# Feed-forward matmuls of a two-layer encoder: from the full array to two 64-row tiles

## The chip, the cores and the metric

One core of a Trainium2 chip runs the whole program in one launch. The metric is device time in microseconds; the kernel before takes 1270.34 us (median of three runs, 1270.18 to 1270.63).

## What is computed

Two encoder layers over 256 tokens of width 1024, in float32. Each layer is a feed-forward half step, a mixer of three attention branches, and a second feed-forward half step:

```python
def swiglu(h, w1, w3, w2):
    return (jax.nn.silu(h @ w1) * (h @ w3)) @ w2
for l in range(DEPTH):                       # DEPTH = 2
    x = x + 0.5 * swiglu(rms_norm(x, ffn1_norm[l]), ffn1_w1[l], ffn1_w3[l], ffn1_w2[l])
    ...                                      # the mixer
    x = x + 0.5 * swiglu(rms_norm(x, ffn2_norm[l]), ffn2_w1[l], ffn2_w3[l], ffn2_w2[l])
```

w1 and w3 are 1024 x 2816, w2 is 2816 x 1024. So there are four feed-forward blocks, and the change touches nothing else.

## The kernel before

**Split products.** TensorE takes float32r operands. To keep float32 accuracy every operand a is split into hi = round(a) and lo = a - hi, and a product is summed as hi*hi + hi*lo + lo*hi. Activations are kept transposed: `xT[:, t, w, k, :]` holds tokens of half t (128 each), w = 0 for hi and 1 for lo, for feature block k.

**The weight stream.** All weights come in units of up to 1 MB, in a fixed order (L74 to L111). A unit goes by DMA from SP's queue into one of three `raw` buffers (L115), ScalarE rounds it to hi in two halves (`emit_hi`, L133, the instruction on L138), VectorE subtracts to get lo (`emit_lo`, L141, the instruction on L144), both into one of four `hl` buffers. `unit()` (L157) hands out the next unit and writes out the splits that are still missing up to the first half of the one behind it; `tick()` (L181), called between bursts of matmuls, writes out the next splits (`fill`, L163, at most two units ahead) and lets each side task take a step. The order of the program text is the order in each engine's queue.

**A feed-forward block** (`ffn`, L448) has 22 units of w1 and w3 (128 columns of each, eight blocks of 128 rows) and then 11 units of w2.
- Units 0 and 1 run with the activations as the stationary operand (`tform`, L451) while the norm is still being finished; their results are transposed by `tr_task` (L462). In the first block of the program `start_first` (L298) does these two units instead.
- Units 2 to 21 run through `fform` (L493): for b = 0 (w1) and b = 1 (w3), and for each of eight k, one matmul with hi weights streams 512 columns (hi and lo of the 256 tokens, L503), and one with lo weights streams 256 columns (hi, L504). The two halves of a PSUM bank collect xhi*whi + xhi*wlo and xlo*whi apart. `rs_bcast` (L290) transposes the norm factors over all partitions after unit 2.
- `fdrain` (L473) evacuates a unit: per bank a ScalarE copy of the upper half (L478) and a VectorE add of the lower (L479), a GpSimd multiplication by the norm factor (L480), then SiLU, gate product and split (L485 to L491).
- `wide_out` (L413) multiplies by w2: for each of the first nine units and each token half t, `wide_burst` (L437) issues 12 matmuls of 512 columns into two banks. Units 9 and 10 are held to the end, so that each of the four banks is finished in turn.

Eight PSUM banks: four tagged `acc`, four tagged `ta` (L69 to L71). `fform` uses two `acc` banks a unit; `wide_out` uses all four.

## Time and profile before

| what | value |
|---|---|
| runs | 1270.34 us median (1270.18 to 1270.63) |
| profiled execution, first to last instruction | 1267.6 us |
| granted TensorE clock | 1.000 over the whole span |
| PE busy / weight loads busy | 1253.1 us / 1074.4 us |
| VectorE / ScalarE / GpSimd busy | 894.0 / 711.9 / 221.3 us |
| read from HBM | 224 MB, 178 GB/s over the span |

The profile gives the span of its execution, not a time of its own beside it; the median of the runs is 2.7 us more than that span, which is what lies ahead of the first and behind the last instruction. Matmuls are pipelined: a row's "busy" overlaps the next one's, so that the pace of TensorE is read from starts and counts, not from durations. "PEld" is the weight load that precedes each matmul.

### The profile page before, as it was taken

To read this page: it belongs to the slowest core of one execution; us is meant where nothing else is said; L and a number is where in the kernel's file an instruction comes from. 1 tells how busy PE (TensorE), PEld (TensorE's weight loads), DVE (VectorE), ACT (ScalarE), POOL (GpSimd) and SP (SyncE) were. 2 spreads that over 40 slices of the span, in tenths; PEclk is the share of its full clock that TensorE was granted. 3 is DMA by queue.
4 is the path that set the end of the run, shared out by engine and by line. 5 is a ranking of instruction groups with operands and counts; after the bars stand their busy time and mean duration, and the time that the engine had idled before them with its cause. 6 is when DMAs were issued, how large, how long until landed. Compare 5 with 4: busy or idle time off the path is not lost.

```text
span 1267.6 us, 18330 instructions
## 1 busy us (share of the span) xinstructions
PE 1253.1 (99%) x7124; PEld 1074.4 (85%) x7124; DVE 894.0 (71%) x1382; ACT 711.9 (56%) x1315; POOL 221.3 (17%) x169
## 2 busy tenths in 40 slices
PE   8999999999999999999999999999999999999998
PEld 7888788889988898888898888888899788988887
DVE  5888736678766878886378886466886567788852
ACT  6555536667665366555365564356686644665541
POOL 0322101132011112220012220021322020122200
PEclk9999999999999999999999999999999999999999
DMA  7655644552543545556355556346526434555561
GB/s 301 222 180 187 241 158 158 203 194 87 196 166 133 200 166 185 185 196 232 133 186 203 195 195 235 113 173 225 167 90 207 163 134 170 196 199 182 186 230 34
DMA packets 37751, 228.34 MB, mean 180 GB/s; under 512 B 5712, under 2 KB 6864, under 8 KB 13088
## 3 DMA queue, kind: packets, MB, share of 16 engines
q1 hardware_dynamic: 37488, 227.09, 50.5%
q8 instruction: 56, 0.92, 0.3%
q14 instruction: 31, 0.25, 0.1%
q0 software_dynamic: 32, 0.07, 0.0%
q10 hardware_dynamic: 144, 0.00, 0.0%
HBM read 224.00 MB, written 1.05 MB: 178 GB/s over the span
## 4 chain that ended last, share of the span: by engine, by line
PE 88%; DVE 7%; ACT 4%; issue 1%; DMA 0%; DVEq 0%; ACTq 0%
PE acc L368 79%; DVE hl L144 6%; PE ta L368 6%; ACT hl L138 2%; ACT s L478 1%; PE ta L689 1%; PE ta L259 1%; DVE s L487 1%; PE ta L776 0%; DVE aT L1017 0%; PE ta L1172 0%; DMA gcol<-in_gcol 0%; PE ta L674 0%; ACT aT L1016 0%; PE ta L608 0%
## 5 line engine op out<-in xcount | busy, mean ns | idle before, releaser
L144 DVE TENSOR_TENSOR hl<-raw,hl 128x1024 fp32r<-128x1024 f32 (+2 forms) x422 | 568.0, 1385 | 101.7 <-ACT hl L138 91.4
L138 ACT ACTIVATE hl<-raw 128x1024 fp32r<-128x1024 f32 (+2 forms) x422 | 417.2, 1041 | 110.2 <-PE acc L368 93.5
L368 PE MATMUL acc<-xT,hl 128*128 128x512 f32 (+1 forms) x2768 | 475.6, 334 | 0.6 <-DVE s L479 0.6
L368 PEld LDWEIGHTS acc<-xT,hl 128*128 128x128 f32 x2768 | 417.8, 188 | 55.7 <-DVE s L479 0.9
L368 PE MATMUL acc<-hl,xT 128*128 128x512 f32 (+2 forms) x1728 | 369.0, 369 | 0.0
L368 PEld LDWEIGHTS acc<-hl,xT 128*128 128x128 f32 x1728 | 299.8, 188 | 45.7 <-issue 2.1
L368 PE MATMUL acc<-hl,s 128*128 128x512 f32 x1344 | 310.9, 391 | 1.5 <-DVE s L479 1.5
L368 PEld LDWEIGHTS acc<-hl,s 128*128 128x128 f32 x1344 | 250.8, 188 | 54.4 <-DVE s L479 1.9
L480 POOL TENSOR_TENSOR s<-s,rsb 128x512 f32<-128x512 f32 x80 | 111.8, 1397 | 355.7 <-DVE s L479 355.7
L489 ACT ACTIVATE s<-s 128x256 fp32r<-128x256 f32 x82 | 34.2, 418 | 172.4 <-DVE s L487 172.4
L479 DVE TENSOR_TENSOR s<-acc,s 128x256 f32<-128x256 f32 x158 | 59.6, 419 | 58.5 <-ACT s L478 58.5
L569 POOL TENSOR_TENSOR sm<-sm,mhalf 128x4 f32<-128x4 f32 (+2 forms) x24 | 36.7, 1531 | 202.7 <-DVE sm L573 196.0
L280 POOL TENSOR_TENSOR sm<-sm,mhalf 128x1 f32<-128x1 f32 x12 | 14.2, 1182 | 298.5 <-DVE sm L279 298.5
L478 ACT ACTIVATE s<-acc 128x256 f32<-128x256 f32 x158 | 50.6, 372 | 0.0
L242 ACT ACTIVATE s<-ta 128x512 fp32r<-128x512 f32 (+1 forms) x46 | 22.9, 531 | 39.9 <-PE ta L689 19.9
L243 DVE TENSOR_TENSOR s<-ta,s 128x512 fp32r<-128x512 f32 (+1 forms) x46 | 26.6, 604 | 24.4 <-ACT s L242 24.1
L368 PE MATMUL ta<-s,s 64*64 64x128 f32 (+3 forms) x720 | 41.0, 265 | 2.1 <-ACT s L1026 2.1
L368 PEld LDWEIGHTS ta<-s,s 64*64 64x64 f32 (+2 forms) x720 | 32.1, 144 | 12.4 <-issue 5.9
L262 ACT ACTIVATE xT<-ta,gain 128x128 fp32r<-128x128 f32 x80 | 22.8, 369 | 35.1 <-PE ta L259 35.1
L485 ACT ACTIVATE s<-s 128x256 f32<-128x256 f32 x82 | 34.2, 418 | 10.9 <-POOL s L480 0.2
L546 DVE SCALAR_TENSOR_TENSOR x<-acc,x 128x512 f32<-128x512 f32 (+1 forms) x20 | 11.3, 579 | 39.7 <-PE acc L368 39.7
L491 DVE TENSOR_TENSOR s<-s,s 128x256 fp32r<-128x256 f32 x82 | 34.0, 415 | 1.9 <-ACT s L489 1.9
(158 smaller groups left out, 652.4 us busy)
## 6 DMA issues: line engine op xcount, KB each, us to landing
raw<-in_l_f_w SPq DMA_DIRECT2D x130, 1024.0 KB, 4.8
raw<-in_l_in_g SPq DMA_DIRECT2D x16, 816.0 KB, 4.4
raw<-in_l_in_late SPq DMA_DIRECT2D x8, 1024.0 KB, 4.8
raw<-in_l_out SPq DMA_DIRECT2D x8, 1024.0 KB, 4.7
raw<-in_l_in_m SPq DMA_DIRECT2D x4, 1024.0 KB, 4.8
raw<-in_l_in_gr SPq DMA_DIRECT2D x4, 1024.0 KB, 4.8
raw<-in_l_in_r SPq DMA_DIRECT2D x4, 1024.0 KB, 4.8
raw<-in_l_in_nv SPq DMA_DIRECT2D x4, 1024.0 KB, 5.0
```

Source lines behind the costliest of these rows:

```text
L138: ACT.activation(out=hls[j][:, 0, sl], in_=raws[j][:, sl], func=AF.Copy)
L144: DVE.tensor_tensor(out=hl[:, 1, sl], in0=r[:, sl], in1=hl[:, 0, sl].bitcast(F32), op=ALU.subtract)
L242: ACT.activation(out=hi, in_=ps, func=AF.Copy)
L243: DVE.tensor_tensor(out=lo, in0=ps, in1=hi.bitcast(F32), op=ALU.subtract)
L368: PE.matmul(out=out, lhsT=lhsT, rhs=rhs, start=start, stop=stop, skip_group_check=True)
L478: ACT.activation(out=g[:, j, :], in_=a[j][:, 256:], func=AF.Copy)
L479: DVE.tensor_tensor(out=g[:, j, :], in0=a[j][:, :256], in1=g[:, j, :], op=ALU.add)
L480: POOL.tensor_tensor(out=g, in0=g, in1=rb[:, None, :].to_broadcast([128, 2, 256]), op=ALU.mult)
L485: ACT.activation(out=g[:, 0, :], in_=g[:, 0, :], func=AF.Silu)
L489: ACT.activation(out=o[:, 0, :], in_=g[:, 0, :], func=AF.Copy)
L491: DVE.tensor_tensor(out=o[:, 1, :], in0=g[:, 0, :], in1=o[:, 0, :].bitcast(F32), op=ALU.subtract)
L569: POOL.tensor_tensor(out=r[:, :n], in0=ss[:, :n], in1=mhalf[:, :n], op=ALU.pow)
```

## The change

`duo` is new. It takes two lists of runs, P and Q. A run is a list of matmuls into one PSUM bank. Each 128-row matmul is cut in two of 64 rows (`HALF`), and the matmuls of P on one half of the rows alternate with those of Q on the other half. After both runs of P and Q are through on their first halves, the halves are exchanged. Since both halves add into the same bank, a GpSimd memset of one element (`dot`) waits for the ends of a pair of first runs, and the pair of second runs into those banks waits for that memset.

`fform_pair` does two units of w1/w3 at a time: P and Q are the two units, with two runs (w1, w3) of 24 matmuls of 256 columns each (three per k), all into one sum of 256 columns. Their four banks alternate between `ta` and `acc`. `fdrain` is then called with both banks as a and b, which leaves out L478, L479 and L480 and multiplies straight from PSUM by the norm factor (L483, L484). In `wide_out`, P and Q are the two token halves, with two runs of six matmuls of 512 columns; the held units stay as they were. The first block keeps `fform` for units 2 and 3. `tr_task` is now finished right behind `rs_bcast` after the first pair.

```diff
+        def duo(P, Q, between=None):
+            gate = {}
+            for second in (False, True):
+                for n, pair in enumerate(zip(*((Q, P) if second else (P, Q)))):
+                    last = [None, None]
+                    for i in range(len(pair[0][0])):
+                        for r in range(2):
+                            ops, start, stop = pair[r]
+                            out, lhsT, rhs = ops[i]
+                            last[r] = mm(out, lhsT[HALF[r]], rhs[HALF[r]], start and not second and i == 0,
+                                         stop and second and i == len(ops) - 1)
+                            if second and i == 0:
+                                tc.add_manual_dep(last[r], gate[n], SYNC, reason="the other row tile's run in this bank")
+                    if not second:
+                        g = POOL.memset(dot[:, n:n + 1], 0.0).ins
+                        for r in range(2):
+                            tc.add_manual_dep(g, last[r].name, SYNC, reason="both row tiles' runs")
+                        gate[n] = g.name
+                    if between is not None and not (second and n == len(P) - 1):
+                        between()
...
@@ wide_out
-                for t in range(2):
-                    if u == 0:
-                        accs[t] = (acc_t(), acc_t())
-                    wide_burst(accs[t], lhs, u, hl, t, u == 0, False)
-                    tick()
+                if u == 0:
+                    for t in range(2):
+                        accs[t] = (acc_t(), acc_t())
+                P, Q = (wide_runs(accs[t], lhs, u, hl, t) for t in range(2))
+                duo(*((Q, P) if u % 2 else (P, Q)), between=tick)
+                tick()
...
+        def wide_runs(acc, lhs, u, hl, t):
+            runs = []
+            for h in range(2):
+                ops = []
+                for kk in range(2):
+                    sl = slice(kk * 1024 + h * 512, kk * 1024 + h * 512 + 512)
+                    for x_, w_ in ((0, 0), (0, 1), (1, 0)):
+                        ops.append((acc[h], lhs(x_, u, kk, t), hl[:, w_, sl]))
+                runs.append((ops, u == 0, False))
+            return runs
...
+            def fform_pair(i):
+                runs, accs = [], []
+                for j in (i, i + 1):
+                    hl = unit()
+                    acc = [at_t() if i // 2 % 2 == 0 else acc_t() for _ in range(2)]
+                    accs.append(acc)
+                    runs.append([])
+                    for b in range(2):
+                        o = acc[b][:, :256].rearrange("p (t n) -> p t n", t=2)
+                        ops = []
+                        for k in range(8):
+                            a = k * 256 + b * 128
+                            for w_, x_ in ((0, 0), (0, 1), (1, 0)):
+                                ops.append((o, hl[:, w_, a:a + 128], xT[:, :, x_, k, :]))
+                        runs[-1].append((ops, True, True))
+                duo(*runs, between=tick)
+                if i == 2:
+                    rs_bcast()
+                    finish(utr)
+                for j in range(2):
+                    drains[i + j] = run(fdrain(i + j, accs[j][0][:, :256], accs[j][1][:, :256]))
+                tick()
...
-            for i in range(2, NB):
-                fform(i)
+            if first is not None:
+                for i in (2, 3):
+                    fform(i)
+            for i in range(2 if first is None else 4, NB, 2):
+                fform_pair(i)
```

How the instructions move on TensorE in the w1/w3 stage: of before, a stretch of one unit (`xT` is the moving operand, `hl` the weights; 512 and 256 are columns):

```order
L368 MATMUL acc<-xT,hl 128x256
L368 MATMUL acc<-xT,hl 128x512 [waits DVE_49]
L368 MATMUL acc<-xT,hl 128x256
L368 MATMUL acc<-xT,hl 128x512
L368 MATMUL acc<-xT,hl 128x256
```

Of the change, one pair of units (the size shown is the output's, all 128 partitions of it; each of these matmuls takes 64 rows):

```order
L367 MATMUL acc<-xT,hl 128x256 [waits Activation_49] x2
L367 MATMUL acc<-xT,hl 128x256 x2
L367 MATMUL acc<-xT,hl 128x256 [waits DVE_49] x2
L367 MATMUL acc<-xT,hl 128x256 x19
L367 MATMUL acc<-xT,hl 128x256 [waits Activation_49]
L367 MATMUL acc<-xT,hl 128x256 x3
L367 MATMUL acc<-xT,hl 128x256 [waits DVE_49]
L367 MATMUL acc<-xT,hl 128x256 x66
L367 MATMUL acc<-xT,hl 128x256 [waits Pool_49]
L367 MATMUL acc<-xT,hl 128x256 x47
L367 MATMUL acc<-xT,hl 128x256 [waits Pool_49]
L367 MATMUL acc<-xT,hl 128x256 x47
```

Before, two units were 64 matmuls; now they are 192, of 256 columns and 64 rows each, in four stretches of 48, the third and fourth of which begin with a wait for GpSimd.

TensorE in the w2 stage of the change, from the middle of a unit's first stretch to its end (s_396 and s_520 are the split gate products of two 128-column blocks):

```order
L367 MATMUL acc<-hl,s_520 128x512 [waits Activation_49]
L367 MATMUL acc<-hl,s_520 128x512
L367 MATMUL acc<-hl,s_520 128x512 [waits DVE_49]
L367 MATMUL acc<-hl,s_520 128x512 x3
L367 MATMUL acc<-hl,s_396 128x512 x6
L367 MATMUL acc<-hl,s_520 128x512 x6
L367 MATMUL acc<-hl,s_396 128x512 [waits Pool_49]
L367 MATMUL acc<-hl,s_396 128x512 x5
L367 MATMUL acc<-hl,s_520 128x512 x6
L367 MATMUL acc<-hl,s_396 128x512 [waits Pool_49]
L367 MATMUL acc<-hl,s_396 128x512 x5
L367 MATMUL acc<-hl,s_520 128x512 x6
```

A unit was 24 matmuls of 128 rows; it is 48 of 64 rows, again in four stretches, of 12 matmuls each, and the third and fourth begin with the wait for GpSimd.

GpSimd in the first block, before:

```order
L280 TENSOR_TENSOR sm<-sm,mhalf 128x1 [waits DVE_49]
L480 TENSOR_TENSOR s_335<-s_335,rsb 128x512 [waits DVE_49]
L480 TENSOR_TENSOR s_397<-s_397,rsb 128x512 [waits DVE_49]
L480 TENSOR_TENSOR s_449<-s_449,rsb 128x512 [waits DVE_49]
L219 MEMSET aT_78 128x512
L219 MEMSET aT_79 128x512
```

and with the change:

```order
L512 TENSOR_TENSOR s_398<-s_398,rsb 128x512 [waits DVE_49]
L393 MEMSET dot 1x1 [waits PE_49] x2
L218 MEMSET aT_78 128x512
L218 MEMSET aT_79 128x512
L393 MEMSET dot 1x1 [waits PE_49,Pool_49] x34
```

The multiplications of the drains are gone but for those of units 2 and 3, and 34 memsets follow each other, each behind matmuls.

## Rows read from the trace of the kernel before

**Rows 1.** The page: busy time by engine, granted clock in 40 slices
```profile
PE 1253.1 (99%) x7124; PEld 1074.4 (85%) x7124; DVE 894.0 (71%) x1382; ACT 711.9 (56%) x1315; POOL 221.3 (17%) x169
...
PEclk9999999999999999999999999999999999999999
```

**Rows 2.** The page: the chain that ended last, by engine
```profile
PE 88%; DVE 7%; ACT 4%; issue 1%; DMA 0%; DVEq 0%; ACTq 0%
```

**Rows 3.** Waits of PE (us in total, times, longest)
```profile
PE ta L368 <- ACT hl L337: 6.0, 1, 6.0
PE ta L368 <- ACT s L1026: 2.1, 2, 1.1
PE acc L368 <- DVE s L479: 2.1, 2, 1.5
PE ta L1172 <- DVE s L1163: 0.4, 2, 0.2
```

**Rows 4.** Windows in the second block's w1/w3 and w2 stages: length, busy (instructions)
```profile
475.00:570.00 95.00, 95.00 (x543) 83.24 (x542) 79.85 (x104) 55.70 (x102) 23.75 (x17) 1.00 0.55 189
580.00:618.00 38.00, 38.00 (x169) 31.47 (x168) 20.70 (x20) 16.28 (x17) 0.00 (x0) 1.00 0.61 224
```

**Rows 5.** Groups by form, 475 to 570 us (busy us, mean ns | idle before)
```profile
L368 PE MATMUL acc<-xT,hl 128*128 128x512 f32 x271 | 95.2, 393 | 0.0
L368 PE MATMUL acc<-xT,hl 128*128 128x256 f32 x272 | 76.9, 283 | 0.0
L144 DVE TENSOR_TENSOR hl<-raw,hl 128x1024 fp32r<-128x1024 f32 x36 | 58.2, 1655 | 2.7 <-ACT hl L138 0.4
...
L480 POOL TENSOR_TENSOR s<-s,rsb 128x512 f32<-128x512 f32 x17 | 23.8, 1397 | 70.6 <-DVE s L479 70.6
L479 DVE TENSOR_TENSOR s<-acc,s 128x256 f32<-128x256 f32 x34 | 12.8, 419 | 12.9 <-ACT s L478 12.9
```

**Rows 6.** Groups by form, 580 to 618 us
```profile
L368 PE MATMUL acc<-hl,s 128*128 128x512 f32 x169 | 38.5, 389 | 0.0
...
L144 DVE TENSOR_TENSOR hl<-raw,hl 128x1024 fp32r<-128x1024 f32 x18 | 22.0, 1270 | 17.0 <-ACT hl L138 16.8
```

**Rows 7.** The chain, 276 to 320 us: start, us, what
```profile
279.67 2.80 PE acc L368 x12
282.46 0.87 PE ta L689 x8
...
307.62 2.85 PE acc L368 x24
```

**Rows 8.** Timeline of row-tiled loads, then matmuls, of the latent attention, cut to windows
```profile
296.33 0.19 PEld L368 LDWEIGHTS ta<-s,s 64*128 64x128 f32 x2
296.33 0.30 PEld L368 LDWEIGHTS ta<-s,s 64*128 64x128 f32 x4
296.33 0.42 PEld L368 LDWEIGHTS ta<-s,s 64*128 64x128 f32 x6
296.55 0.41 PE L368 MATMUL ta<-s,s 64*128 64x256 f32 x4
```

**Rows 9.** Groups by form, PE and PEld, whole span
```profile
L368 PE MATMUL ta<-s,s 64*128 64x256 f32 x48 | 5.0, 312 | 0.0
...
L368 PEld LDWEIGHTS acc<-hl,s 128*128 128x128 f32 x1344 | 250.8, 188 | 54.4 <-DVE s L479 1.9 <-issue 0.7
L368 PEld LDWEIGHTS ta<-s,s 64*128 64x128 f32 x48 | 3.4, 185 | 1.1
```

**Rows 10.** Timeline of four 64 x 64 tiles (linear attention), windows ended one round later
```profile
380.11 0.56 PE L368 MATMUL ta<-s,s 64*64 64x128 f32 x12
380.11 0.67 PE L368 MATMUL ta<-s,s 64*64 64x128 f32 x16
```

**Rows 11.** The chain around the 64 x 64 tiles, 378 to 388 us
```profile
380.78 2.97 PE acc L368 x12
383.75 0.82 PE ta L368 x24
```

**Rows 12.** Groups by form, POOL, whole span: the smallest memset
```profile
L300 POOL MEMSET ones<- 128x1 f32 x1 | 0.1, 98 | 0.0
```

More of the change, by code (lines that the diff above doesn't have):

```diff
@@ L28 @@
 S2_BUFS = 31
-FIRST_R = 2
 ROW = {}
@@ L367, in mm @@
         def mm(out, lhsT, rhs, start, stop):
-            PE.matmul(out=out, lhsT=lhsT, rhs=rhs, start=start, stop=stop, skip_group_check=True)
+            return PE.matmul(out=out, lhsT=lhsT, rhs=rhs, start=start, stop=stop, skip_group_check=True).ins
+        HALF = (slice(0, 64), slice(64, 128))
+        dot = cst.tile([1, 4], F32, name="dot")
+        SYNC = mybir.DependencyInfo(mybir.DependencyClass.Sync, mybir.DependencyReason.DATA)
+        def duo(P, Q, between=None):
[18 more added lines that the diff above has]
+                        between()
         def burst(acc, lh, hl, ks, t, N, start, stop, k0=0):
@@ L435, in wide_out @@
                     tick(True)
-        def wide_burst(acc, lhs, u, hl, t, start, stop):
-            for kk in range(2):
-                s, e = start and kk == 0, stop and kk == 1
-                for w in range(2):
-                    for h in range(2):
-                        mm(acc[h], lhs(0, u, kk, t), hl[:, w, kk * 1024 + h * 512:kk * 1024 + h * 512 + 512],
-                           s and w == 0, False)
-                for h in range(2):
-                    mm(acc[h], lhs(1, u, kk, t), hl[:, 0, kk * 1024 + h * 512:kk * 1024 + h * 512 + 512], False, e)
+        def wide_runs(acc, lhs, u, hl, t):
[8 more added lines that the diff above has]
+            return runs
         def ffn(norms, after, prefetch, first=None, out=None):
@@ L494, in fform @@
                 hl = unit()
-                acc = [(at_t() if first is not None and i == 3 else acc_t()) for _ in range(2)]
+                acc = [(at_t() if i == 3 else acc_t()) for _ in range(2)]
                 for b in range(2):
@@ L504, in fform @@
                         tick()
-                if i == (FIRST_R if first is not None else 2):
+                if i == 2:
                     rs_bcast()
-                    if first is not None:
-                        for j in range(2):
-                            drains[j] = run(fdrain(j, first[j][0][:, :256], first[j][1][:, :256]))
-                        for j, a in held:
-                            drains[j] = run(fdrain(j, a))
-                if "x" in rs_b:
-                    drains[i] = run(fdrain(i, acc))
-                else:
-                    held.append((i, acc))
-                tick()
-            us, drains, held = {}, {}, []
+                    for j in range(2):
+                        drains[j] = run(fdrain(j, first[j][0][:, :256], first[j][1][:, :256]))
+                drains[i] = run(fdrain(i, acc))
+                tick()
+            def fform_pair(i):
[14 more added lines that the diff above has]
+                duo(*runs, between=tick)
+                if i == 2:
+                    rs_bcast()
+                    finish(utr)
+                for j in range(2):
+                    drains[i + j] = run(fdrain(i + j, accs[j][0][:, :256], accs[j][1][:, :256]))
+                tick()
+            us, drains = {}, {}
             if first is None:
@@ L526, in ffn @@
                         tick(t == 0)
-                utr = spawn(tr_task(us), 2)
-            for i in range(2, NB):
-                fform(i)
+                utr = spawn(tr_task(us), 99)
+            if first is not None:
[3 more added lines that the diff above has]
+                fform_pair(i)
                 if i == 4:
@@ L533, in ffn @@
                         load_consts()
-                    if first is None:
-                        finish(utr)
             def lhs(hl, u, kk, t):
```

## Prediction

> **What bounds the kernel now.** [...] Busy PE is not yet PE at its pace, so the next view is what PE waits for: 10.6 us in all, of which 6.0 us at the start, and 2.1 us behind the drains of w1/w3 in the feed-forward [rows 3]. TensorE is bound by its own instruction stream; only a shorter stream helps.
>
> Its pace comes from counts. Of the records that touch a window, about two began before it. In the w1/w3 stage 95 us hold some 541 starts [rows 4], half of them of 512 and half of 256 columns [rows 5]: 0.1756 us each, 5.62 us for a unit's 32 matmuls and **11.24 us for two units**. In the w2 stage 38 us hold some 167 starts [rows 4], all of 512 columns [rows 6]: **0.227 us each**. [...]
>
> **The change, part by part.**
>
> *w1/w3 in pairs.* A unit's columns stay the same (512 + 256 become 256 + 256 + 256), but three loads take the place of two in each k. A pair of units becomes 96 slots, each of two half-height matmuls side by side. If both tiles of a slot run at once, a pair costs 96 slots. The latent attention already has this very form: float32r, 64 rows, 128 weight columns, 256 moving columns, 48 records [rows 9], in two tiles. Its loads cover 0.19 us for the first two, 0.30 us for four and 0.42 us for six [rows 8]: the two tiles begin within 0.01 us (one load lasts 0.185 us [rows 9]), and the third slot adds 0.12 us. The last four matmuls cover 0.41 us [rows 8], of which the last alone is some 0.28 us (the full-array form has 0.283 [rows 5]), which leaves 0.13 us for one slot and the lag of the second tile. So the tiles do run at once, and a slot takes 0.12 us, rounded; I take 0.119, as the full array has it at 256 columns. Hence 96 x 0.119 = 11.42 us against 11.24: +0.18 us a pair. There are 9 pairs in the first block and 10 in each of the others, 39 in all: **+7.2 us**. The bounds of a slot are 0.109 us, the step of one round of the four 64 x 64 tiles (0.67 - 0.56 = 0.11 [rows 10]), and 0.13 us, the upper end of the rounding; each 0.005 us is worth 96 x 39 x 0.005 = 18.7 us.
>
> *w2 in tiles.* 24 slots of 512 columns take the place of 24 matmuls, in 9 units of 4 blocks: 864. No row shows two tiles at 512 columns. [...]
>
> [...] The rows show that the full array loads its next weights under the running matmul: a load lasts 0.188 us [rows 9], yet loads of which one belongs to each matmul follow at 0.119 us. [...]
>
> *Changing between full height and half height.* A group of 12 matmuls takes 2.80 us in a row of its kind [rows 7] and 2.97 us right behind 64-row tiles; six rounds of those take 0.82 us behind full matmuls instead of 6 x 0.109 = 0.65 [rows 11]. So 0.17 us a change. The first block changes twice (into the pairs, out into the held units), the others four times, as the transposes behind the first pair are of full height: 14 x 0.17 = **+2.4 us**.
>
> *The gates.* Each waits for a pair of runs, and there is one more pair of runs between it and the instruction that it holds: 24 slots (2.9 us) in w1/w3, 6 slots (1.36 us) in w2. A memset takes 0.098 us [rows 12]. With the tail of a matmul (0.389 us long [rows 6], begun 0.227 before the next run) and two hops between engines it comes to some 0.5 us, so I cost it at nothing; its cover is those 1.36 us. GpSimd's queue holds little else then: in the first block two `aT` memsets and a drain of unit 3, inside 2.9 us of cover and more.
>
> *The shorter drains.* Per unit, 2 ScalarE copies, and 1.40 us of GpSimd leave [rows 5]; VectorE keeps as many operations. Its splits take 1.66 us beside GpSimd's multiplications and 1.27 without [rows 5, 6]. VectorE would do 4 x 1.27 + 8 x 0.42 = 8.4 us of the 11.4 of a pair: off the path. The wait behind drains disappears, since pairs alternate between bank groups: **-2.1 us** [rows 3]. Late next is the second unit of the first pair, whose splits are wanted at the pair's start rather than half a pair later: one split, 1.3 us, call it **+1.1 us** (0 to 3.3). In three blocks the second pair's bank waits for the evacuation of the norm factors: 3 x 0.2 = **+0.6 us**.
>
> Sum: 7.2 + 0 + 2.4 - 2.1 + 1.1 + 0.6 = +9.2 us on a span of 1267.6, 1276.8. The median of the runs is 2.7 us above that span, and I leave this as it is: **1279.5 us**, 0.7% slower. A measurement here tells about 0.2% (2.5 us) from no change.
>
> **The rivals.**
>
> [...]
>
> [...]
>
> *The gates stall.* If a memset's round trip took over 1.36 us, 72 gates in w2 would each pay the rest; at 2 us 72 x 0.64 = 46 us. The 0.098 us of a memset speaks against it.
>
> *The tiles take turns.* Then slots double and w1/w3 alone costs some 400 us. Starts within 0.01 us exclude it [rows 8].
>
> **How the numbers follow.** Forecast, slots at 0.117 to 0.121 us and w2 within 3 us of now: 0.48, 1273 to 1288. All slots at the floor: 0.18. One stage or a part of it gains, net faster (1250 to 1267): 0.14; net the same: 0.10. Issue-bound or gates: 0.10. So faster 0.32, same 0.10, slower 0.58. Likeliest is the forecast, 1279.5. The range that leaves out no more than 2 in 10 goes from 1237 to 1293: it cuts off the floor's own time and the issue-bound case.
>
> **What would show it.** In the profile after, the w1/w3 stage should have some 0.06 us between starts, two within 0.01 us, and 11.4 us a pair; w2 slots of 0.227 us; no L478 or L480 in the pairs, splits near 1.3 us; a PE wait for the memsets of nearly nothing; 14 gaps of 0.2 us at the changes of height. A slot under 0.117 us in long runs, or 0.216 us at 512 columns, makes the prediction wrong on the fast side; stretches over 11.9 us a pair, or PE waiting for POOL, on the slow side.

## Result and the profile after

The changed kernel takes 1287.83 us (median of four runs, 1287.77 to 1287.88) against 1270.26 us in the runs beside it: **1.4% slower, ratio 1.0142 (95% interval 1.0129 to 1.0155)**. The forecast was 1279.5 us with a range of 1237 to 1293, so its sign and its likeliest case came, at twice the size. The profiled spans are 1286.0 us after and 1267.6 before: 18.4 us to explain. The part ahead of the prediction puts the 2.7 us between the median before and this span down to what lies outside the instructions. After, the difference is 1.9 us, and among the runs beside e10 an execution of before that took 1269.43 us has the same span, so some 0.8 us of the 2.7 came from comparing two executions.

The page of the kernel after, engines and granted clock (before: [rows 1]):

```profile
PE 1270.4 (99%) x13076; PEld 1157.7 (90%) x13076; DVE 821.9 (64%) x1382; ACT 661.4 (51%) x1159; POOL 127.1 (10%) x249
...
PEclk9999999999999999999999999999999999999999
```

The evacuation did become cheaper: VectorE gave up 72 us, ScalarE 50 and GpSimd 94, the last over two fifths of its work. None of it set TensorE's pace: TensorE stays busy from end to end at a granted clock of 1.000, with 13076 matmuls in place of 7124.

What PE waits for, after (us in total, times, longest; before: [rows 3]):

```profile
PE ta L367 <- ACT hl L336: 5.5, 2, 5.2
PE ta L367 <- DVE hl L143: 2.4, 1, 2.4
PE ta L367 <- ACT s L1077: 2.0, 2, 1.0
PE ta L367 <- DVE s L511: 0.4, 1, 0.4
PE acc L367 <- DVE hl L143: 0.4, 1, 0.4
PE ta L1223 <- DVE s L1214: 0.4, 2, 0.2
PE ta L367 <- DVE hl L342: 0.2, 1, 0.2
```

The 2.1 us for the evacuation are gone. New are 2.4 us for weight splits (L143) and 0.4 for the evacuation (L511) in the first pair. The other 0.4 us for L143 lie in the first two units, at 15 us, where no pair runs; e4 and e12 have them too, and in both kernels these two units are over at the same time (last start at 20.6 us). No line names POOL: the gates hold nothing up. The waits come to 11.3 us in all, against 10.6. What grew is the stream itself.

Windows in the second block's w1/w3 and w2 stages, after (us; busy us and instructions of PE, PEld, DVE, ACT, POOL; granted clock; DMA share; GB/s), to be read against [rows 4]:

```profile
483.00:578.00 95.00, 95.00 (x1588) 95.00 (x1586) 62.88 (x103) 45.48 (x70) 1.50 (x17) 1.00 0.50 179
590.00:628.00 38.00, 38.00 (x339) 35.87 (x338) 19.91 (x19) 15.55 (x16) 1.23 (x14) 1.00 0.62 222
```

Some four records began ahead of each window, so 95 us hold 1584 starts, 0.0600 us each. Taken from first to last start of nine pairs it is 60.02 ns (1728 starts, 481.98 to 585.64 us): **a slot of two takes 0.1200 us and a pair 11.52 us**, against 11.24 before. In w2 38 us hold 335 or 336 starts, 0.1132 us each: 0.2263 us a slot, where a full-height matmul took 0.2268.

Timeline of PE in the w1/w3 stage, cut to windows that end 0.1 us apart:

```profile
499.83 0.65 PE L367 MATMUL acc<-xT,hl 64*128 64x256 f32 x8
499.83 0.77 PE L367 MATMUL acc<-xT,hl 64*128 64x256 f32 x10
499.83 0.89 PE L367 MATMUL acc<-xT,hl 64*128 64x256 f32 x12
```

Two matmuls come with each 0.12 us. Their single starts lie 0.006 to 0.015 us apart, then 0.110 us pass until the next two. The tiles run side by side, as forecast, and a slot gains nothing by it.

The groups by form of after, 483 to 578 us (busy us, mean ns | idle before), and then the group of the gates' memsets over the whole span:

```profile
L367 PEld LDWEIGHTS ta<-xT,hl 64*128 64x128 f32 x818 | 49.5, 185 | 0.0
...
L143 DVE TENSOR_TENSOR hl<-raw,hl 128x1024 fp32r<-128x1024 f32 x33 | 39.6, 1220 | 9.9 <-ACT hl L137 9.9
```

```profile
L393 POOL MEMSET dot<- 1x1 f32 x158 | 13.9, 88 | 661.5 <-PE acc L367 441.1 <-PE ta L367 220.4
```

A split takes 1.22 us in place of 1.66 [rows 5] now that GpSimd does not multiply beside it (1.56 in e1, where it does again), and a gate's memset 0.088 us.

**A correction.** The part ahead of the prediction says that the change touches only the four feed-forward blocks. That is wrong: `wide_out` is also the mixers' output projection, and two of its units in each mixer run in half-height tiles too. The timeline of PE there shows it, of after:

```profile
432.24 0.60 PE L1223 MATMUL ta<-idt,s 128*128 128x128 f32 x4
432.77 1.67 PE L367 MATMUL acc<-hl,xT 64*128 64x512 f32 x12
434.37 0.66 PE L1223 MATMUL ta<-idt,s 128*128 128x128 f32 x4
434.96 12.41 PE L367 MATMUL acc<-hl,xT 64*128 64x512 f32 x93
```

The mixers grew by 1.75 and 1.65 us, which the forecast had at nothing. Block by block, from the starts in both traces (0.3 us of block 4 lie behind its last matmul):

| stage | growth, us | slots of w1/w3 | height changes | rest |
|---|---|---|---|---|
| block 1 | +4.0 | 9 x 0.28 = 2.5 | out of the pairs: 0.2 | first pair +3.8 (with the change of height into it), evacuation -2.6 |
| mixer 1 | +1.75 | | 4 x 0.2 = 0.8 | about 0.9 (e4) |
| block 2 | +3.5 | 10 x 0.28 = 2.8 | 0.8 | w2 -0.1 |
| block 3 | +3.6 | 2.8 | 0.8 | w2 -0.1 |
| mixer 2 | +1.65 | | 0.8 | about 0.8 (e4) |
| block 4 | +3.8 | 2.8 | 0.8 | w2 -0.1, behind the last matmul +0.3 |

The first pair takes 15.29 us from its first start to the next pair's, where the others take 11.52; 2.8 of these 3.8 us are the two waits in it. Before, the evacuation's two waits of 0.57 and 1.49 us make one unit take 6.35 us in place of 5.62, and 240 starts of the w2 stage 56.05 us in place of 54.2 (as in the second block), together 2.6.

The experiments ask whether these entries are what they are called.

### The profile page after: what moved, and what is told of

Read it like the earlier page. It is cut to its first block, busy times and chain, and to the rows that moved or that the text cites. A ratio compares the mean times of both kernels' runs of the same rounds, so it can differ in the third digit from the quotient of the medians.

```text
span 1286.0 us, 30350 instructions
## 1 busy us (share of the span) xinstructions
PE 1270.4 (99%) x13076; PEld 1157.7 (90%) x13076; DVE 821.9 (64%) x1382; ACT 661.4 (51%) x1159; POOL 127.1 (10%) x249
## 4 chain that ended last, share of the span: by engine, by line
PE 95%; DVE 2%; ACT 1%; DMA 1%; issue 0%; SPq 0%; DVEq 0%; ACTq 0%
PE acc L367 69%; PE ta L367 23%; DVE hl L143 1%; PE ta L740 1%; ACT hl L137 1%; PE ta L258 1%; DMA raw<-in_l_f_w 1%; PE ta L827 0%; DVE aT L1068 0%; PE ta L1223 0%; PE ta L725 0%; DVE s L519 0%; ACT aT L1067 0%; PE ta L293 0%; PE ta L659 0%
## 5 line engine op out<-in xcount | busy, mean ns | idle before, releaser
L143 DVE TENSOR_TENSOR hl<-raw,hl 128x1024 fp32r<-128x1024 f32 (+2 forms) x422 | 502.6, 1224 | 138.1 <-ACT hl L137 137.8
L367 PE MATMUL acc<-hl,xT 128*128 128x512 f32 (+3 forms) x1824 | 371.4, 371 | 0.0
L367 PEld LDWEIGHTS acc<-hl,xT 128*128 128x128 f32 (+1 forms) x1824 | 299.9, 188 | 48.7 <-issue 3.5
L367 PE MATMUL acc<-hl,s 64*128 64x512 f32 (+1 forms) x2208 | 311.5, 388 | 0.0
L367 PEld LDWEIGHTS acc<-hl,s 64*128 64x128 f32 (+1 forms) x2208 | 268.5, 185 | 35.6 <-issue 2.1
L367 PE MATMUL acc<-xT,hl 64*128 64x256 f32 (+2 forms) x3920 | 259.0, 280 | 0.4 <-DVE hl L143 0.4
L367 PE MATMUL ta<-xT,hl 64*128 64x256 f32 (+2 forms) x3920 | 250.0, 280 | 8.5 <-ACT hl L336 5.5
L367 PEld LDWEIGHTS acc<-xT,hl 64*128 64x128 f32 (+1 forms) x3920 | 254.7, 185 | 2.0 <-DVE hl L143 0.6
L367 PEld LDWEIGHTS ta<-xT,hl 64*128 64x128 f32 (+1 forms) x3920 | 245.3, 185 | 11.2 <-ACT hl L336 5.7
L516 DVE TENSOR_TENSOR s<-ta,rsb 128x256 f32<-128x256 f32 x41 | 17.2, 420 | 45.2 <-PE ta L367 45.2
L516 DVE TENSOR_TENSOR s<-acc,rsb 128x256 f32<-128x256 f32 x39 | 16.3, 419 | 39.6 <-PE acc L367 39.6
L597 DVE SCALAR_TENSOR_TENSOR x<-acc,x 128x512 f32<-128x512 f32 (+1 forms) x20 | 11.3, 580 | 40.6 <-PE acc L367 40.6
```

The costliest lines, as they stand in the source:

```text
L143: DVE.tensor_tensor(out=hl[:, 1, sl], in0=r[:, sl], in1=hl[:, 0, sl].bitcast(F32), op=ALU.subtract)
L367: return PE.matmul(out=out, lhsT=lhsT, rhs=rhs, start=start, stop=stop, skip_group_check=True).ins
L516: DVE.tensor_tensor(out=g[:, 1, :], in0=b, in1=rb, op=ALU.mult)
```

## The experiments

### Tiles or the third pass: e1, e2 and e5

e1 keeps the tiles and takes the third pass away, with the old evacuation that two sums need:

```diff
 fform_pair
-                        o = acc[b][:, :256].rearrange("p (t n) -> p t n", t=2)
+                        o = acc[b].rearrange("p (w t n) -> p w t n", w=2, t=2)
...
-                            for w_, x_ in ((0, 0), (0, 1), (1, 0)):
-                                ops.append((o, hl[:, w_, a:a + 128], xT[:, :, x_, k, :]))
+                            both = xT[:, :, :, k, :].rearrange("p t w n -> p w t n")
+                            ops.append((o, hl[:, 0, a:a + 128], both))
+                            ops.append((o[:, 0], hl[:, 1, a:a + 128], xT[:, :, 0, k, :]))
...
-                    drains[i + j] = run(fdrain(i + j, accs[j][0][:, :256], accs[j][1][:, :256]))
+                    drains[i + j] = run(fdrain(i + j, accs[j]))
```

> The changed kernel with w1/w3 again in two passes (512 and 256 columns) but still in two 64-row tiles, with the old evacuation. Third load (my theory): a load adds about 13 ns to its tile's stream whether the array is tiled or not, so 32 slots of 512 and 32 of 256 columns take the 11.24 us of before instead of 11.53, 39 times 0.28 us less than the changed kernel: 1277 us, ratio 1.005. Tiles as such are slow: the pair stays near 11.5 us and the time near 1288. The evacuation matters: VectorE's splits go back to 1.6 us and the pair gets longer than 11.5.

Measured: 1288.97 us (1286.35 to 1293.14), ratio 1.0145 (1.0128 to 1.0162). The pairs did come down to 11.27 us (88.07 ns a start, 128 starts), but nothing was left of it at the end. The theory's 13 ns for a load were the author's estimate; measured are 11.52 - 11.27 = 0.25 us for 32 slots more, 8 ns each. PE's waits in e1, from the slowest of its four executions:

```profile
PE acc L367 <- POOL dot L393: 7.2, 4, 1.8
...
PE ta L367 <- POOL dot L393: 0.9, 3, 0.3
```

At the start of each of the four w2 stages PE stands 1.8 us before a gate. The memsets themselves last no longer; two of them stand in GpSimd's queue behind the evacuation's products of a pair's two units, which take 3.50 us together. The timeline of GpSimd and then of PE at the second block's w2 stage, and then windows behind it (columns as above), of e1:

```profile
585.60 3.50 POOL L512 TENSOR_TENSOR s<-s,rsb 128x512 f32<-128x512 f32 x2 [6.35 <-DVE s L511]
589.05 0.12 POOL L393 MEMSET dot<- 1x1 f32 x2
```

```profile
589.19 11.00 PE L367 MATMUL acc<-hl,s 64*128 64x512 f32 x80 [1.80 <-POOL dot L393]
```

```profile
589.50:592.00 2.50, 2.50 (x18) 1.96 (x16) 2.12 (x5) 1.50 (x4) 0.00 (x0) 0.65 0.24 49
592.00:594.00 2.00, 2.00 (x14) 1.58 (x12) 1.72 (x2) 1.30 (x3) 0.00 (x0) 0.59 0.94 393
594.00:606.00 12.00, 12.00 (x110) 11.16 (x108) 5.46 (x6) 5.10 (x6) 0.35 (x4) 1.00 0.70 240
```

Behind the wait the granted clock falls to 0.65 over 2.5 us and 0.59 over the next 2. Eight slots then take 0.427 us in place of 0.227, 1.6 us. So one late gate costs 1.8 + 1.6 us in this execution, and the four stages 13.6. The fall does not come in every execution: the fastest, 1286.35 us, ran at a granted clock of 1.000 and has a span 6.8 us shorter, about four such falls. This is the rival of the stalled gates, in its place and with a price that the forecast had not: it fell silent in the change itself because the shorter evacuation leaves those products out of GpSimd's queue.

e5 tests that reading by moving the product alone:

```diff
 e1's fdrain
-                    POOL.tensor_tensor(out=g, in0=g, in1=rb[:, None, :].to_broadcast([128, 2, 256]), op=ALU.mult)
+                    DVE.tensor_tensor(out=g, in0=g, in1=rb[:, None, :].to_broadcast([128, 2, 256]), op=ALU.mult)
```

> e1's kernel (512- and 256-column passes in two row tiles, the long evacuation) with the evacuation's product with the norm factor on VectorE in place of GpSimd, so that no 1.4 us product stands ahead of the gates' memsets in GpSimd's queue. Theory (e1 lost its gain to late gates, not to its passes): w1/w3 pairs of 11.27 us as in e1, no PE wait for GpSimd, w2 slots back at 0.2263 us, TensorE's granted clock 1.00 through the w2 stages; against the changed kernel only the third weight load is gone, 39 x (11.52 - 11.27) = 9.8 us: 1278, ratio 1.006. Rival (the shorter evacuation is also needed because VectorE gets late with a longer one): the weight splits L143 come late, PE waits for them or for the accumulators in blocks 2 to 4, and the time stays at 1284 to 1290.

Measured: 1276.56 us (1275.73 to 1276.62), ratio 1.0052 (1.0038 to 1.0066), 1.4 us from the expectation. PE waits for POOL's `dot` nowhere, and the w2 stage is back at a granted clock of 1.00. Windows of e5 in the w1/w3 and w2 stages:

```profile
483.00:578.00 95.00, 95.00 (x1088) 82.24 (x1088) 76.72 (x122) 55.67 (x104) 1.53 (x17) 1.00 0.53 188
590.00:628.00 38.00, 38.00 (x340) 35.87 (x338) 17.46 (x15) 14.32 (x15) 1.25 (x14) 1.00 0.63 222
```

From first to last start a pair is 128 x 87.57 ns = 11.21 us, where the full height has 11.24. Even these 0.03 us are not the tiles': `dot` moves the buffers by 32 bytes, and e4 (below), at full height with its buffers in the same places, has 509 starts from 478 to 567 us, 175.0 ns each: 64 of them, two units, take 11.20 us. Its window in that stage, to be read against the 543 records of before [rows 4]:

```profile
475.00:570.00 95.00, 95.00 (x545) 82.97 (x544) 79.61 (x104) 56.38 (x103) 23.78 (x18) 1.00 0.53 180
```

Place for place the tiles gain nothing in w1/w3. VectorE carries the product without being missed (871.9 us busy).

e2 is the counterpart: three passes and the short evacuation at full height, no tiles.

```diff
 before, fform
-                    o = acc[b].rearrange("p (w t n) -> p w t n", w=2, t=2)
+                    o = acc[b][:, :256].rearrange("p (t n) -> p t n", t=2)
...
-                        mm(o, hl[:, 0, a:a + 128], both, k == 0, False)
-                        mm(o[:, 0], hl[:, 1, a:a + 128], xT[:, :, 0, k, :], False, k == 7)
+                        mm(o, hl[:, 0, a:a + 128], xT[:, :, 0, k, :], k == 0, False)
+                        mm(o, hl[:, 0, a:a + 128], xT[:, :, 1, k, :], False, False)
+                        mm(o, hl[:, 1, a:a + 128], xT[:, :, 0, k, :], False, k == 7)
...
-                    drains[i] = run(fdrain(i, acc))
+                    drains[i] = run(fdrain(i, acc[0][:, :256], acc[1][:, :256]))
```

> The kernel before with w1/w3 in three passes of 256 columns at full height and the short evacuation, no tiles. Third load: 48 matmuls of 0.120 us, 5.76 us a unit instead of 5.62, 80 units: +11 us, less the 2.1 us of waits behind drains: 1279 us, ratio 1.007; with the changed kernel at 1288 the other 9 us would be height changes, the first block and the mixer. Tiles are the cost: no slower than before, 1268 to 1270 us.

Measured: 1276.35 us (1276.13 to 1276.64), ratio 1.0053 (1.0038 to 1.0068). The window of e2 in the second block's w1/w3 stage:

```profile
470.00:565.00 95.00, 95.00 (x794) 95.00 (x793) 65.30 (x104) 46.37 (x69) 0.00 (x0) 1.00 0.51 179
```

Some 792 starts in 95 us are 0.120 us each (120.00 ns from 470 to 577 us), the slot of the tiles to the digit, and the third and fourth block have the same. So the 0.28 us that a pair of units costs more there belongs to the third pass and not to the tiles. The evacuation waits are gone here too (block 1 is 2.0 us shorter), and what remains over the kernel is three blocks of 2.8 us. The first block is an exception that stays open: its matmuls take 118.7 ns in e2 and 120.0 a slot in tiles, 1.2 us over nine pairs.

### What holds a slot at 0.12 us: e8

```diff
 duo's w1/w3 matmuls
-                                ops.append((o, hl[:, w_, a:a + 128], xT[:, :, x_, k, :]))
+                                for tt in range(2):
+                                    ops.append((o[:, tt], hl[:, w_, a:a + 128], xT[:, tt, x_, k, :]))
```

> The changed kernel with each 256-column w1/w3 matmul of the tiled pairs as two of 128 columns with the same weights (384 starts a pair in place of 192). What makes a slot of two tiles 0.120 us at 256 columns is asked. If it is the columns plus a fixed remainder (0.1063 us for 256 columns, from the difference of the 512- and 256-column slots, 0.2263 and 0.1200, so 0.0137 over): a slot of 128 columns takes 0.067 us, a pair 12.8 us, the kernel +51 us, about 1338. If it is the two weight loads of a slot (0.06 us each): slots stay at 0.12 us, a pair takes 23.0 us, +449 us, about 1737. If it is a pace of starts of about 0.06 us each, the same 1737, and the loads' own records then tell: PEld busy near full means the loads, with room in it the starts.

Measured: 1851.22 us in one run. Its window in the third block's w1/w3 stage:

```profile
1050.00:1145.00 95.00, 95.00 (x1707) 95.00 (x1704) 35.93 (x56) 25.10 (x38) 0.88 (x10) 1.00 0.34 119
```

1701 starts in 95 us are 55.8 ns each. Half the columns, and a slot only goes from 0.1200 to 0.1117 us. From 35 to 407 us, nearly the whole w1/w3 stage of the first block, the granted clock was down (0.50 in the window of 40 to 400 us), so the time of the whole is not compared with the expectation's, and a start took 0.1067 us there, a slot 0.2133:

```profile
40.00:400.00 360.00, 360.00 (x3378) 360.00 (x3378) 65.60 (x104) 44.71 (x69) 2.52 (x20) 0.50 0.16 56
```

The time of a slot went with the granted clock: 0.2133 us at 0.50, 0.1117 at 1.00. At 1.00 a pair of 64-row matmuls with a load each did not follow the last at less than 0.1117 us, with half the columns, and what fills that time is one of two things that e8 doesn't part: two loads of 128 weight columns one behind the other, or two starts. The expectation wanted PEld's busy share to tell; it is full in either case, as the records of 0.188 us overlap each other, so this stays open. Two things follow all the same. At 256 columns a slot is above this floor (0.1200 against 0.1117), which leaves, by elimination, its columns and what a matmul takes beside them as what holds it; what comes beside the columns is 2 x 0.1200 - 0.2263 = 0.0137 us by the change's two slots, an estimate. And a slot of 0.109 us, the prediction's lower bound, was not seen with these loads: it lies under this floor.

### Heights and places: e3, e4 and e13

e3 leaves w1/w3 of the change alone and puts `wide_out` back to `wide_burst`, for w2 and for the output projection:

```diff
 after, wide_out
...
-                P, Q = (wide_runs(accs[t], lhs, u, hl, t) for t in range(2))
-                duo(*((Q, P) if u % 2 else (P, Q)), between=tick)
-                tick()
+                    wide_burst(accs[t], lhs, u, hl, t, u == 0, False)
+                    tick()
```

> The changed kernel with the wide output stage (w2, and the mixer's output projection, which runs through the same function) at full height again. If 512-column slots in tiles cost what full matmuls cost (0.2263 against 0.2268 us): +0.4 us there, and less 8 height changes in the two mixers (8 times 0.17 = 1.4 us): 1286.8 us, ratio 1.013. If the tiled output stage is behind the mixer's growth as a whole (1.7 us a mixer): 1284.

Measured: 1286.51 us (1285.63 to 1286.72), ratio 1.0131 (1.0116 to 1.0146): 1.3 us under the change, where two mixers were expected to give back 1.4 less 0.4 in w2. The total is not a clean measure: in e3's profiled execution the granted clock falls behind the first pair's wait (0.72 from 35 to 41 us, 1.00 in the change), and its first block is 0.5 us longer. So the output projection is read by itself. The timeline of the same place in e3, against the rows of after above:

```profile
432.71 0.60 PE L1220 MATMUL ta<-idt,s 128*128 128x128 f32 x4
433.07 3.04 PE L367 MATMUL acc<-hl,xT 128*128 128x512 f32 x12
435.95 0.60 PE L1220 MATMUL ta<-idt,s 128*128 128x128 f32 x4
```

Behind four transposes a full-height matmul starts 0.36 us after the first of them, a half-height one 0.53 us. From the first of these transposes to the next block's first matmul, with four changes of height between, both mixers take 25.32 us in the change and 24.54 in e3: 0.79 us, 0.2 us a change.

e4 adds to the kernel before nothing but the 16 bytes of `dot`, which move `raw`, `hl`, `s2` and all behind them by 32 bytes:

```diff
 before
+        dot = cst.tile([1, 4], F32, name="dot")
+        POOL.memset(dot, 0.0)
```

> The kernel before with the 16-byte tile dot allocated and set once, nothing else; it moves the weight buffers and all scratch tiles by 32 bytes. If the place of the buffers is what makes the mixer's 512-column matmuls 235.5 instead of 233.7 ns a piece: those become 235.5 here too and the time 1271.5 to 1272 us, ratio 1.001. If it is the order of work around them: 233.7 ns and 1270.3 us.

Measured: 1271.55 us (ten runs, 1269.81 to 1273.01) against 1269.73, ratio 1.0014 (1.0004 to 1.0023). The chain of waits gives the same 60 dense matmuls of the first mixer (start us, us, what), of before, of e4 and of after:

```profile
200.68 13.94 PE acc L368 x60
```

```profile
202.45 14.04 PE acc L371 x60
```

```profile
204.68 14.05 PE acc L367 x60
```

An unused tile of 16 bytes slows them by 0.1 us, 1.8 ns each, and the change shows the same pace. With 1056 such matmuls of 512 columns in the kernel that is 1.9 us, and by the starts e4's two mixers are 1.2 and 0.95 us longer than those of before. That the whole grew by 1.8 us is partly chance, and not the evidence: its w1/w3 units became shorter (5.60 us, 0.4 us in each later block), and in the profiled execution the first block's evacuation wait was 1.7 us in place of 1.5, with a fall of the granted clock behind it:

```profile
139.00:145.00 6.00, 6.00 (x20) 4.77 (x20) 4.86 (x6) 3.73 (x6) 1.34 (x1) 0.72 0.57 194
```

e13 then asks whether the tiled slot follows places too. It is the change with `am`, `gcol`, `mhalf` and `ones` allocated ahead of `xT` and `dot` in the room that `ones` leaves (the places of e10, below):

```diff
 after
+        am = cst.tile([128, 64], I32, name="am")
+        gcol = cst.tile([128, 8], F32, name="gcol")
+        mhalf = cst.tile([128, 16], F32, name="mhalf")
+        od = cst.tile([128, 8], F32, name="od")
+        ones, dot = od[:, :1], od[:1, 4:8]
         xT = cst.tile([128, 2, 2, 8, 128], F32R, name="xT")
...
-        dot = cst.tile([1, 4], F32, name="dot")
```

> The changed kernel with its small tiles laid as in e10: am, gcol, mhalf and ones ahead of xT, and the gates' 16 bytes inside the room that ones leaves, so that hl, raw and s2 lie where they lie in the kernel before. Taken from e10's paces: the dense 512-column matmuls fall from 235.5 to 228.9 ns in the mixers and the first units, some 4 us over the kernel with what else e10 showed there. Theory A (the tiled slot also follows xT's place, as the full-height pass of 512 and 256 columns did, 351.5 to 347.1 ns): slots of 0.1200 us go to about 0.1185, 39 x 96 x 0.0015 = 5.6 us more, 1278. Theory B (the 256-column slot does not move): 0.1200 as before, 1283 to 1284. Either way it stays above the kernel before with the same places (1263.3), as a third load at full height cost 6 us in e2.

Measured: 1283.45 us (1282.76 to 1284.0), ratio 1.0105 (1.0088 to 1.0122). The same window of its w1/w3 stage:

```profile
483.00:578.00 95.00, 95.00 (x1588) 95.00 (x1586) 63.42 (x101) 46.29 (x70) 1.46 (x18) 1.00 0.50 179
```

1588 records, as in the change (60.02 ns a start in both): theory B. The tiled slot of 256 columns does not move with the places, the dense matmuls do, and so do the tiled slots of 512 columns in the output projection (0.234 us in the change, 0.227 here). The change with the best places known here is still above the kernel before without them, and some 20 us above the kernel before with them (e10, below): the full-height w1/w3 units gain by the places, the tiled ones do not.

### The first pair's wait: e12

```diff
 after, ffn and fform
-                for i in (2, 3):
+                for i in range(2, 6):
                     fform(i)
-            for i in range(2 if first is None else 4, NB, 2):
+            for i in range(2 if first is None else 6, NB, 2):
...
-                if i == 4:
+                if i == (4 if first is None else 6):
...
-                acc = [(at_t() if i == 3 else acc_t()) for _ in range(2)]
+                acc = [(at_t() if i % 2 else acc_t()) for _ in range(2)]
```

> The changed kernel with the first feed-forward block's units 4 and 5 at full height too, one unit after the other, and its tiled pairs only from unit 6. In the changed kernel PE waits 2.4 us in one piece for the splits of VectorE (L143) in the first pair of that block (a pair works on two units at once, so it needs the second unit's weights a unit earlier) and 0.4 and 0.4 us for them and for L511 behind it. Theory (that wait belongs to a pair that meets weights still on their way, and is over once the stream is ahead): it goes, 2.4 to 3.2 us less, 1284.5 to 1285.5. Rival (the stream is not ahead by unit 6 either): PE waits as long there, within 0.7 us of 1287.8.

Measured: 1288.48 us (1288.4 to 1288.68), ratio 1.0145 (1.013 to 1.016). The theory fell. The timeline of PE around the first pair, of after and of e12:

```profile
35.23 2.90 PE L367 MATMUL ta<-xT,hl 64*128 64x256 f32 x43 [2.39 <-DVE hl L143]
38.55 1.67 PE L367 MATMUL ta<-xT,hl 64*128 64x256 f32 x19 [0.43 <-DVE s L511]
```

```profile
44.67 0.51 PE L367 MATMUL acc<-xT,hl 64*128 64x256 f32 x4 [1.08 <-ACT hl L137]
46.79 1.60 PE L367 MATMUL acc<-xT,hl 64*128 64x256 f32 x18 [1.61 <-DVE hl L143]
```

The wait moves with the pair: 1.1 + 1.6 us at unit 6 in place of 2.4 + 0.4 us at unit 4. The full-height units before it have not let the splits get ahead. The pair takes two units at its start, so once in the program it asks for a unit early; that `unit()` and `fill` write splits out no more than two units ahead fits this, but was not varied. The pair itself takes 16.3 us in place of 15.3, as the granted clock falls behind the second wait (0.69 from 46.5 to 52 us). So the cost came with the first pair at both places tried, and was not that of the kernel's start.

### A version that beats both: e9, e10 and e11

e4 had shown that places count, so e9 moved the other operand of the dense matmuls:

```diff
 before
-S2_BUFS = 31
+S2_BUFS = 30
...
+        pad0 = cst.tile([128, 96], F32, name="pad0")
         xT = cst.tile([128, 2, 2, 8, 128], F32R, name="xT")
...
         zT = cst.tile([32, 2, 256], F32R, name="zT")
+        pad1 = cst.tile([128, 32], F32, name="pad1")
...
```

> The kernel before with 384 bytes ahead of xT and 128 behind zT (and one s2 buffer fewer, to make the room): xT then begins at a multiple of 1024 bytes (25600, from 25216), and hl stays at a multiple of 512 (90624, from 90112). e4 showed that 32 bytes of shift in hl make a dense 512-column matmul 235.5 ns in place of 233.7, while the w2 ones, whose weights lie in s2, take 226.7. Theory A (the excess over 226.7 is how the two operands lie to each other, and aligning both takes it away): dense and w1/w3 512-column matmuls go towards 227 ns, w1/w3 units from 5.62 to about 5.5 us, 5 to 11 us less, 1259 to 1265. Theory B (the excess belongs to what runs in xT's place or to the other engines' accesses, not to its address): 233 to 236 ns as before, 1269 to 1272.

Measured: 1270.66 us (1269.4 to 1271.67), ratio 1.0008 (0.9999 to 1.0017). The paces were those of theory A (229 ns dense, 5.55 us for a w1/w3 unit), the time that of theory B. PE's waits in e9 say where it went:

```profile
PE ta L678 <- ACT s L913: 4.4, 2, 2.2
```

This wait is not among those of before, and behind each of its two pieces the granted clock falls. Windows of e9:

```profile
311.00:317.00 6.00, 5.15 (x22) 4.69 (x23) 5.89 (x11) 5.77 (x15) 0.96 (x1) 0.72 0.11 32
939.00:945.00 6.00, 5.75 (x26) 5.42 (x25) 5.89 (x13) 4.72 (x11) 1.99 (x2) 0.72 0.19 44
```

Each mixer of e9 is 3.9 us longer than that of e10 (below): 2.2 for the wait and 1.7 for the clock. That is all of the 7.7 us by which the two spans differ. e10 gets the room without giving up an `s2` buffer, by the order of allocation alone:

```diff
 before
+        am = cst.tile([128, 64], I32, name="am")
+        gcol = cst.tile([128, 8], F32, name="gcol")
+        mhalf = cst.tile([128, 16], F32, name="mhalf")
+        ones = cst.tile([128, 1], F32, name="ones")
         xT = cst.tile([128, 2, 2, 8, 128], F32R, name="xT")
...
-        am = cst.tile([128, 64], I32, name="am")
...
-        gcol = cst.tile([128, 8], F32, name="gcol")
-        mhalf = cst.tile([128, 16], F32, name="mhalf")
-        ones = cst.tile([128, 1], F32, name="ones")
```

> The kernel before with four small constant tiles (am, gcol, mhalf, ones: 384 bytes) allocated ahead of xT in place of behind it: xT begins at 25600, a multiple of 1024 bytes, and raw, hl, s2 and all behind them lie where they lay, with all 31 s2 buffers. e9 made dense 512-column matmuls 228.9 ns (from 233.7) and a w1/w3 unit 5.55 us (from 5.62), some 6 us over the kernel, and lost as much in the mixers, where PE waited 4.4 us more for ScalarE's L913. Theory A (that loss was the missing s2 buffer, the pace was xT's place): the same paces, without the wait for L913, 1263 to 1266. Theory B (hl's place made the pace in e9): 233 to 236 ns as before, 1269 to 1272. Theory C (a faster dense stage only moves the mixers' attention chains later against PE): the paces of e9, and the waits of the mixers with them, 1269 to 1271.

Measured: **1263.3 us (1262.38 to 1263.94), ratio 0.9950 (0.9937 to 0.9964)**. The wait for L913 is gone, and the pace stays. The chain's 60 dense matmuls in e10, where before had 13.94 us, and then its window in the w1/w3 stage, where 95 us of before hold 543 records:

```profile
200.53 13.66 PE acc L368 x60
```

```profile
470.00:565.00 95.00, 95.00 (x551) 83.03 (x550) 79.51 (x103) 56.37 (x106) 23.73 (x17) 1.00 0.52 180
```

Only `xT` (and the tiles between it and `zT`) lies elsewhere, 384 bytes further, at a multiple of 1024. Theory A holds, with the qualification that e9's loss may have come from the missing buffer or from `hl`'s place, which e10 put back together.

e11 adds other banks for every odd unit of the first block, the one thing of the change that took a wait away:

```diff
 e10, fform
-                acc = [(at_t() if first is not None and i == 3 else acc_t()) for _ in range(2)]
+                acc = [(at_t() if first is not None and i % 2 else acc_t()) for _ in range(2)]
```

> e10 with every second unit of the first feed-forward block (all odd ones, not the third alone) in the other four PSUM banks, so that a unit's banks are those of two units before it. It takes away the 2.1 us for which PE waits for VectorE's evacuation in the first block (rows of the kernel before), which the full-height three-pass kernel e2 also lost with its other banks. Theory: 2 us under e10. Rival (the unit after it then waits for its weights): as e10 within 0.5 us.

Measured: **1259.31 us (1259.01 to 1259.66), ratio 0.9920 (0.9906 to 0.9933)**, the fastest of all. What PE still waits for in e11:

```profile
PE ta L368 <- ACT hl L337: 6.2, 1, 6.2
PE ta L368 <- ACT s L1026: 2.4, 2, 1.2
PE ta L689 <- DVE s L824: 0.5, 2, 0.2
PE ta L1172 <- DVE s L1163: 0.4, 2, 0.2
```

The evacuation's line is gone. It gave 4.0 us where 2 were expected: 2.6 in the first block's w1/w3 stage (608 starts at 173.6 ns in place of 177.9, now as in the other blocks) and 1.4 in its w2 stage (240 starts at 226.9 in place of 232.7, its wait of 1.0 us included). The listed waits of e10, 1.8 us, are less than half of it. Most of the rest is pace and not waiting: behind its wait e10's first block takes 5.66 us a unit, its other blocks and all of e11's 5.55. Why the other banks bring that back is not settled.

## Why the prediction was right, and where its sum was off

**The bound was right.** TensorE's stream sets the time: PE is busy for 99% of the span before and after. 72 us of VectorE, 50 of ScalarE and 94 of GpSimd were taken away and nothing was gained but two waits of 2.1 us, which e11 loses as well by other banks alone, with the long evacuation.

**w1/w3, the term that was mis-sized most.** The forecast took 0.119 us for a slot, from 24 matmuls of 256 columns in 2.85 us, and got +7.2 us. The slot is 0.1200, and 39 x (11.52 - 11.24) is +11. One nanosecond in 3744 slots is 3.7 us, so the row had to be good to the nanosecond, and it is not a pace: the chain's piece begins at 307.62 us [rows 7], 0.25 us behind the first of these 24 starts. By their starts, 307.37 to 310.18 us in the trace of before, they are 122 ns apart. The reason given for it held: two tiles take what the full array takes at 256 columns, as e2's 0.1200 us at full height shows.

**w2: right.** 0 forecast; 864 x (0.2263 - 0.2268) = -0.4 us. No row of before shows two tiles at 512 columns, so the 0 was the author's estimate; the change showed 0.2263 us a slot.

**Changes of height: the size right, the count wrong.** 0.17 us was taken and 0.2 measured (e3), but there are 22 of them, not 14, because the mixers' output projection was overlooked: 4.4 us in place of 2.4.

**The gates: right for this change, and only for it.** Nothing was forecast and nothing is seen. The prediction's estimate of 0.5 us for a gate took in two hops between engines for which it had no row; in the change's w2 stage a memset began at 592.87 us, 0.51 us behind the start of the last matmul it waits for, and ended 0.37 us into its 1.36 us of cover. But the cover was named as 1.36 us of TensorE's work, and what fills GpSimd's queue ahead of a memset was looked up only in the first block. e1 shows what two products of 3.5 us there do, with a fall of the clock on top that the forecast's 46 us for stalled gates did not contain.

**Evacuation waits: right**, -2.1 us forecast, -2.1 by the rows and -2.6 by the starts. **The norm factors' bank**, +0.6 us, did not come: no PE wait for it stands among the rows of after.

**The first pair: the mechanism right, the size low.** +1.1 us was taken from a range of 0 to 3.3. The rows have 2.4 + 0.4 = 2.8, the starts 3.8 with the change of height, so 3.6, above that range. The wait is for the splits, as forecast, and e12 shows that it goes where the pair goes.

**Placement was not seen at all.** `dot` costs the dense stages of the mixers some 1.8 us by its place alone (e4).

Together 11 - 0.4 + 4.4 - 2.6 + 3.6 + 1.8 = 17.8 us, against 17.6 of the medians and 18.4 of the profiles. Of the 8.6 us beyond the forecast's 9.2 the slot brought 3.8; the first pair (2.5), the changes of height (2.0) and placement (1.8) brought more between them. That the time still lies inside the range is partly luck, since the range was made from bounds of the slot and not for these.

**The rivals.** No run shows the floor that the chances and the range name, nor the 0.216 us at 512 columns, nor an issue-bound case: a slot of the change took 0.1200 us and 0.2263, e8's with half the columns 0.1117, and a matmul at 0.0600 us is held for a hundred microseconds on end, at 0.0558 in e8. Nor did two tiles as such gain: e5 does the same passes in two tiles and takes 11.21 us a pair, where e4 at full height, in the same places, takes 11.20. Tiles that take turns are excluded by the starts, 0.006 to 0.015 us apart.

## What to carry to other kernels

Two half-height tiles won nothing here (11.21 us a pair in e5) over a full-height stream (11.20 in e4) whose loads of 0.188 us [rows 9] already lay under matmuls that start 0.175 us apart, and a third pass cost 0.28 us a pair (e2); before rewriting for tiles, compare the pace per column with and without, over hundreds of starts and to the nanosecond, since small errors are multiplied by thousands. Take a pace from starts and not from a piece of the chain. Count every caller of a shared routine, and price the queue in which a synchronising instruction must stand, not the instruction (0.088 us a memset, 1.8 us of waiting behind products in e1). Try the order of allocation: moving four small tiles, and other banks for one block, gave 0.8% here for no instruction at all.

## What was not expected of the hardware

- A matmul's pace moved with the place of its operands in SBUF. Dense 512-column matmuls took 233.7 ns in the kernel before, 235.5 with `hl` and all behind it 32 bytes further (e4), 228.9 with `xT` 384 bytes further (e10); w1/w3 units went from 5.62 to 5.60 and 5.55 us, while 256-column half-height slots stayed at 0.1200 us (e13). Which property of the addresses does it was not settled, and it is not all: the first blocks of e2 (118.7 ns a matmul, later 120.0) and e10 (5.66 us a unit, later 5.55) run at another pace than their later ones with the same tiles.
- A PE wait of 1.8 us cost nearly as much again in one execution: in e1 the granted clock was 0.65 and 0.59 in the stretches behind it, eight slots of 0.427 us. The length of a wait alone did not tell whether the clock falls: the first pair's wait of 2.4 us in the change was followed by a granted clock of 1.00, the same wait in e3 by 0.72 from 35 to 41 us, and the wait of 1.6 in e12 by 0.69.
- In half-height tiles that alternate, with a load of 128 weight columns each, 0.0558 us was the least time per matmul at a granted clock of 1.00, at 128 columns, and 0.1067 at 0.50 (e8).
